# The last layer's down projection by token rows, with the final norm done along rows

## The chip, the cores and the metric

The kernel runs on one core of a Trainium2 chip. The metric is the device time of one execution in microseconds (us). An execution is profiled separately: the profiler records every instruction of every engine, and the pages quoted here come from one such execution. The engines are called as the profile calls them: PE (TensorE) multiplies matrices, PEld is its loading of the stationary operand, DVE is VectorE, ACT is ScalarE, POOL is GpSimd, SP is SyncE, which here only issues transfers. A q behind a name (SPq, ACTq, POOLq) is that engine's instruction queue.

## The reference

Two layers of a token mixer (three branches, merged by gates) and a gated MLP with a causal convolution, then one RMS norm. For this case only the end matters. S = 512 tokens, D = 1024 features, 2816 hidden columns, all float32:

```python
for l in range(DEPTH):                      # DEPTH = 2
    ...
    x = x + jnp.sum(gates * proj, axis=2) @ w_out[l]
    x = x + conv_ffn(rmsnorm(x, norm2_g[l]), ffn_w_up[l], ffn_conv_w[l], ffn_conv_b[l], ffn_w_down[l])
return rmsnorm(x, final_g)

def rmsnorm(x, g):
    y = x * lax.rsqrt(jnp.mean(x * x, axis=-1, keepdims=True) + EPS) * g
```

`conv_ffn` multiplies by the up weights (1024 to 5632 columns), convolves over three tokens, forms silu(gate) * value (2816 columns) and multiplies by the down weights (2816 to 1024).

## The kernel before

**Layout.** Activations are kept feature-major: a tile has 128 features on the partitions and 512 tokens along the row, so the residual x is eight tiles `x[0..7]`. A matrix product keeps float32 accuracy by three products: each factor is split into a high part (a cast by ACT) and a low part (a subtraction by DVE), and `mm3` (L146 to L157, with the products at L151) issues high x low, high x high and low x high into one PSUM bank. Weights arrive as units of 128 x 512 numbers, 256 KB, by SP's queue into three raw buffers (`load`, L117); `part` (L125) splits them: ACT casts at L134 (tile `sh` or `wh`), DVE subtracts at L135 (`sl` or `wl`). Units are loaded and split ahead of their use: `AHEAD` allows two to five units, by the pool that the split unit goes to. There are 31 "u" buffers, 16 "r" buffers and 39 "f" buffers of 256 KB, and PSUM has two groups of four banks, `acc` and `sm`. A unit feeds 12 products of 512 columns.

**Order.** A scheduler sets each engine's order from the program as written, except where `keep_in_program_order` (`po` in the listing) or `pin` holds it.

**The last layer's end.** `wout` (L1010) computes the residual's tiles one after the other (L1018), splits their normalised form for the up projection and sums their squares (`norm_sq`, L213). `ffn_up` (L1025) takes 22 pairs of columns (gate and value), 24 products each column: DVE evacuates the bank at L1040, ACT and DVE convolve (L1042 to L1044), ACT's tanh and two DVE steps form the activation, and its split at L1052 and L1053 gives the tile pair `ah` (high, low), which goes to an "f" buffer for the first 39 tiles and to an "r" buffer for the last five. `ffn_down` (L1057) takes one output tile of 128 features at a time: 22 slices of the weights are stationary, the activations' 512 tokens move, 66 products in all, then DVE adds half the product to the residual (L1067; the activations are kept doubled) and the squares are summed (L215, L217). In the last layer this goes for tiles 0 to 6.

`finish` (L1078) does tile 7 in two halves of 256 tokens, 66 products of 256 columns each, and interleaves the final norm with them. The squares were added up over tiles 0 to 6 per partition; tiny products with a column of ones sum them over the partitions (L1138 for those tiles, L1107 for tile 7). ACT takes the root (L1109), DVE the reciprocal (L1110); that gives a factor for each token, on the partitions. TensorE turns the factors into rows (L1118), and then eight tiles are multiplied by gain and factor (L1132 on DVE; in the second half two of them at L1130 on GpSimd, with the gain put in earlier by ACT) and stored in 16 pieces of 128 KB (L1133), by SP's and ACT's queues. The first half's multiplications and stores run under the second half's products; the second half's stand alone after the last product.

**Turning.** `turned` (L220) is used by the token mixer for another tile: DVE transposes 32 x 32 blocks (L222), the result is stored to DRAM (`trip`, L227), and four transfers of 64 KB read it back so that rows and columns of blocks are exchanged too (L225).

Of the kernel before, what the change touches and what calls it, by code (L numbers as in the profile page):

```python
# [32 lines left out]
for _n, _w in (("n1", 8), ("mu", 14), ("kk", 4), ("ka", 4), ("a0", 4), ("w0", 4), ("rk", 4), ("lg", 4), ("lb", 4),  # L33
               ("n2", 8), ("cw0", 44), ("cw1", 44), ("cw2", 44), ("cb", 44), ("fg", 8), ("sg", 4), ("sb", 4)):
    PC[_n] = _o
    _o += _w
# [11 lines left out]
class Emit:  # L48
# [251 lines left out]
    def run(self):  # L300
        nc, tc, a, V = self.nc, self.tc, self.a, self.nc.vector
# [9 lines left out]
        st = self.norm_new()  # L311
# [713 lines left out]
    def ffn_up(self, l, st):  # L1025
        nc, V, A = self.nc, self.nc.vector, self.nc.scalar
        nt = [0]

# [28 lines left out]
    def ffn_down(self, l, act, x, st):  # L1057
        nc, V = self.nc, self.nc.vector
        if l < L - 1:
            self.load_pc(l + 1)  # L1060
        xd = []
        for m in range(8):
            if l == L - 1 and m == 7:
                break
            ps = self.acc()
            self.matF(ps, ("wdn", l, m, 0), act)
            V.scalar_tensor_tensor(x[m], ps, 0.5, x[m], op0=MUL, op1=ADD)  # L1067
            if l < L - 1:
                self.norm_z(st, x[m], "n1")
            self.norm_sq(st, x[m])  # L1070
            if l < L - 1:
                d = self.dp.tile([128, 512], F32, name=self.nm("xd"))
                nc.gpsimd.dma_start(d, x[m])
                xd.append(d)
        return x, xd


    def finish(self, l, act, x, acc):  # L1078

        nc, V, A, T = self.nc, self.nc.vector, self.nc.scalar, self.nc.tensor  # L1080
        self.pool = "u"
        w = [self.unit("wdn", l, 7, k * 512, min(512, DFF - k * 512)) for k in range(6)]
        po = self.tc.keep_in_program_order
        pt = self.sm((128, 4))
        hs = [slice(0, 256), slice(256, 512)]
        pss, gx = [self.acc((128, 256)) for _ in range(2)], []

        def prod(h, k0, k1):
            for k in range(k0, k1):
                ks = slice(k % 4 * 128, k % 4 * 128 + 128)  # L1090
                (wh, wl), (xh, xl) = w[k // 4], act[k]
                self.mm3(pss[h], (wh[:, ks], wl[:, ks]), (xh[:, hs[h]], xl[:, hs[h]]), k == 0, k == NFF - 1)

        def square(h):

            sq = self.u((128, 256), n="sq")
            for e in range(2):
                es = slice(128 * e, 128 * e + 128)
                xi = x[7][:, 256 * h + 128 * e:256 * h + 128 * e + 128]
                po(V.scalar_tensor_tensor(xi, pss[h][:, es], 0.5, xi, op0=MUL, op1=ADD))  # L1100
                po(A.activation(sq[:, es], xi, AF.Square))
            return sq

        def stats(h, sq):
            for e in range(2):
                c = 2 * h + e
                po(T.matmul(pt[:, c:c + 1], sq[:, 128 * e:128 * e + 128], self.c("ones"), start=False, stop=True, skip_group_check=True))  # L1107
            ms, rs = self.small((128, 2), "ms"), self.small((128, 2), "rs")
            po(A.activation(ms, pt[:, 2 * h:2 * h + 2], AF.Sqrt, scale=1.0 / D, bias=self.c("eps")))  # L1109
            po(V.reciprocal(rs, ms))  # L1110
            return rs

        def out(h, rs):

            pb = [self.sm((128, 256)) for _ in range(1 + h)]
            for p in pb:
                for e in range(2):
                    po(T.transpose(p[:, 128 * e:128 * e + 128], rs[:, e:e + 1].to_broadcast([128, 128]), self.c("ident")))  # L1118
            return pb

        def scale(h, pb):

            if gx:
                pbs = self.u((128, 256), n="pbs")
                po(A.copy(pbs, pb[1]))
            order = (0, 2, 1, 3, 4, 5, 6, 7) if gx else range(8)
            for j in order:
                t = self.u((128, 256), n="o")
                if gx and j < 2:
                    nc.gpsimd.tensor_tensor(t, gx[j], pbs, op=MUL)  # L1130
                else:
                    po(V.scalar_tensor_tensor(t, x[j][:, hs[h]], self.p("fg", j), pb[0], op0=MUL, op1=MUL))  # L1132
                (nc.scalar if j in (1, 4, 6) else nc.sync).dma_start(self.a["out"][:, j, hs[h]], t)  # L1133

        self.pin = True
        prod(0, 0, 8)
        for c in range(NC):
            po(T.matmul(pt[:, c:c + 1], acc[:, 128 * c:128 * c + 128], self.c("ones"), start=c == 0, stop=False, skip_group_check=True))  # L1138
        prod(0, 8, NFF)
        sq = square(0)  # L1140
        prod(1, 0, 4)
        rs = stats(0, sq)
        prod(1, 4, 8)
        pb = out(0, rs)
        scale(0, pb)
        for j in range(2):
            t = self.u((128, 256), n="gx")
            A.activation(t, x[j][:, hs[1]], AF.Copy, scale=self.p("fg", j))
            gx.append(t)
        prod(1, 8, NFF)  # L1150
        rs = stats(1, square(1))
        scale(1, out(1, rs))

# [55 lines left out]
def _layout(i):  # L1209
    wall, wdn, pcols = [], [], []  # L1210
    for l in range(L):
        w = i["w_in"][l]
# [8 lines left out]
        for j in range(3):  # L1221
# [4 lines left out]
        wdn.append(_chunks(i["ffn_w_down"][l]))  # L1226
# [3 lines left out]
             "cb": i["ffn_conv_b"][l], "fg": i["final_g"], "sg": i["sg_ln_g"][l], "sb": i["sg_ln_b"][l]}  # L1230
# [5 lines left out]
        "wall": np.stack(wall), "wdn": np.stack(wdn), "pcols": np.stack(pcols),  # L1236
# [30 lines left out]
```

## Time and profile before

| what | us |
|---|---|
| median of 3 runs (lowest to highest) | 1719.29 (1718.9 to 1719.91) |
| the profiled execution's own time | 1719.05 |
| its span, first to last instruction | 1717.3 |
| PE busy | 1703.7 |
| DVE busy | 1152.7 |
| ACT busy | 772.5 |
| POOL busy | 147.3 |
| last layer's up projection | about 1358 to 1585 |
| last layer's down projection, tiles 0 to 6 | about 1585 to 1690 |
| tile 7 and the final norm | 1690 to 1717.3 |

Times within the profile count from the start of the span. A row of a group of instructions gives line, engine, operation, output and inputs with their shapes, the count, the busy time and the mean in ns, and then the idle time ahead of them with what ended it. A row of the timeline gives start, duration, and in brackets the idle time before it. The granted clock of TensorE was 0.998 of full speed in the mean. The chip's other cores are not used.

### The profile page before, as it was taken

What the parts mean: (1) busy time and instruction counts of PE and PEld (TensorE: products, weight loads), DVE (VectorE), ACT (ScalarE), POOL (GpSimd) and SP (SyncE); (2) the same over time, 40 slices, a digit from 0 to 9 for tenths busy, and PEclk for the clock granted to TensorE, in tenths of its full rate; (3) what the DMA queues carried; (4) which work ended last, traced back from release to release, by engine and by line L of the source; (5) the groups of instructions that cost most, each with busy time, mean ns of one, the idle gap of its engine ahead of it and who ended that gap; (6) DMA issues with size and microseconds to landing.
All of it is one profiled execution on the core that took longest, in us unless ns stands there. A gap on an engine that the chain in (4) does not pass through costs nothing.

```text
span 1717.3 us, 27555 instructions
## 1 busy us (share of the span) xinstructions
PE 1703.7 (99%) x10368; PEld 1397.7 (81%) x10368; DVE 1152.7 (67%) x1980; ACT 772.5 (45%) x1308; POOL 147.3 (9%) x163
## 2 busy tenths in 40 slices
PE   9999999999999999999999999999999999999997
PEld 7888777788888888888888887778888888888887
DVE  6887745578569777753377886565776787776433
ACT  6563433554255444343265634345433544443322
POOL 2121000013200000000021300000131000000000
PEclk9999999999999999999999999999999999999999
DMA  5236543625443333243332365445254333322332
GB/s 180 87 110 204 172 150 123 184 87 171 149 148 98 98 97 95 72 118 110 115 111 80 122 215 173 132 143 171 89 189 146 125 98 97 99 98 65 107 96 83
DMA packets 132324, 214.89 MB, mean 125 GB/s; under 512 B 16352, under 2 KB 39136, under 8 KB 132192
## 3 DMA queue, kind: packets, MB, share of 16 engines
q1 hardware_dynamic: 117344, 180.67, 34.4%
q10 hardware_dynamic: 10368, 17.78, 2.9%
q0 software_dynamic: 4480, 14.68, 2.6%
q8 instruction: 81, 1.33, 0.3%
q14 instruction: 51, 0.42, 0.1%
HBM read 185.81 MB, written 27.26 MB: 124 GB/s over the span
## 4 chain that ended last, share of the span: by engine, by line
PE 87%; DMA 5%; DVE 4%; ACT 1%; issue 1%; SPq 1%; ACTq 0%; POOL 0%; DVEq 0%; POOLq 0%
PE acc L151 81%; DMA wr<-wall 2%; PE sm L639 2%; DVE wl L135 1%; PE sm L884 1%; PE sm L546 1%; SPq L225 1%; DMA tr<-qkt 1%; DMA tr<-bkT 1%; DMA ws<-sgw 1%; PE sm L989 0%; DMA bkS<-tr 0%; DMA tab<-rot 0%; DVE cs L765 0%; ACT sh L134 0%
## 5 line engine op out<-in xcount | busy, mean ns | idle before, releaser
L151 PE MATMUL acc<-hi,sh 128*128 128x512 f32 x1108 | 431.8, 390 | 0.0
L151 PE MATMUL acc<-lo,sh 128*128 128x512 f32 x1108 | 431.6, 390 | 0.0
L151 PE MATMUL acc<-hi,sl 128*128 128x512 f32 x1108 | 430.5, 390 | 0.0
L134 ACT CAST sh<-wr 128x512 fp32r<-128x512 f32 (+1 forms) x389 | 236.2, 611 | 403.1 <-PE acc L151 305.6
L135 DVE TENSOR_TENSOR sl<-wr,sh 128x512 fp32r<-128x512 f32 (+1 forms) x389 | 262.4, 678 | 185.6 <-PE acc L151 91.5
L151 PEld LDWEIGHTS acc<-lo,sh 128*128 128x128 f32 x1108 | 208.0, 188 | 43.9 <-issue 0.9
L151 PEld LDWEIGHTS acc<-hi,sh 128*128 128x128 f32 x1108 | 208.0, 188 | 43.4 <-issue 0.3
L151 PEld LDWEIGHTS acc<-hi,sl 128*128 128x128 f32 x1108 | 208.0, 188 | 43.4 <-DVE gth L1004 0.3
L151 PE MATMUL acc<-lo,wh 128*128 128x512 f32 x588 | 231.9, 394 | 0.7 <-ACT wh L134 0.4
L151 PE MATMUL acc<-hi,wl 128*128 128x512 f32 x588 | 230.4, 392 | 0.7 <-DVE wl L135 0.6
L151 PE MATMUL acc<-hi,wh 128*128 128x512 f32 x588 | 229.3, 390 | 0.0
L135 DVE TENSOR_TENSOR wl<-wr,wh 128x512 fp32r<-128x512 f32 x195 | 137.9, 708 | 125.2 <-ACT wh L134 122.3
L151 PE MATMUL acc<-ah,sh 128*128 128x512 f32 (+1 forms) x748 | 219.5, 377 | 0.0
L134 ACT CAST wh<-wr 128x512 fp32r<-128x512 f32 x195 | 120.4, 619 | 214.5 <-PE acc L151 145.9
L151 PEld LDWEIGHTS acc<-ah,sh 128*128 128x128 f32 x748 | 137.6, 188 | 25.8
L151 PE MATMUL acc<-ah,sl 128*128 128x512 f32 (+1 forms) x374 | 140.8, 376 | 0.0
L151 PEld LDWEIGHTS acc<-hi,wl 128*128 128x128 f32 x588 | 110.4, 188 | 27.5 <-DVE wl L135 3.8
L151 PEld LDWEIGHTS acc<-lo,wh 128*128 128x128 f32 x588 | 110.3, 188 | 25.5 <-ACT wh L134 1.1
L151 PEld LDWEIGHTS acc<-hi,wh 128*128 128x128 f32 x588 | 110.4, 188 | 22.3 <-issue 0.2
L1040 DVE TENSOR_TENSOR fu<-acc,rsF 128x512 f32<-128x512 f32 x88 | 60.7, 690 | 70.2 <-PE acc L151 70.1
L1042 ACT ACTIVATE cv<-fu,pc 128x512 f32<-128x512 f32 x88 | 71.6, 816 | 41.3 <-DVE fu L1040 37.0
L151 PEld LDWEIGHTS acc<-ah,sl 128*128 128x128 f32 x374 | 70.4, 188 | 12.8
(295 smaller groups left out, 2079.1 us busy)
## 6 DMA issues: line engine op xcount, KB each, us to landing
wr<-wall SPq DMA_DIRECT2D x488, 256.0 KB, 2.6
wr<-wdn SPq DMA_DIRECT2D x80, 256.0 KB, 2.7
gd<-gth ACTq DMA_DIRECT2D x48, 256.0 KB, 3.0
gth<-gd POOLq DMA_DIRECT2D x48, 256.0 KB, 3.5
tr<-bkT SPq DMA_DIRECT2D x16, 256.0 KB, 3.2
bkS<-tr SPq DMA_DIRECT2D x128, 32.0 KB, 2.4
tr<-vT SPq DMA_DIRECT2D x8, 256.0 KB, 2.6
Vt<-tr SPq DMA_DIRECT2D x32, 64.0 KB, 2.3
```

Of the source, the lines that this page charges most:

```text
L134: self.kept(self.nc.scalar.copy(hi[:, :n], raw[:, :n]))
L135: self.kept(self.nc.vector.tensor_tensor(lo[:, :n], raw[:, :n], hi[:, :n], op=SUB))
L151: i = self.nc.tensor.matmul(*x, **y)
L225: q.dma_start(o[32 * f:32 * f + 32, :].rearrange("d (a x) -> d a x", a=4), d[:, f * 128:f * 128 + 128].rearrange("(a d) x -> d a x", d=32))
L546: i = T.matmul(pK[hv[1 - h], j, :], bk[hv[h], c, 1, :], x[hv[h], c, :], start=True, stop=True)
L639: po(T.matmul(o, l, r, start=start, stop=True, skip_group_check=True))
L884: po(T.matmul(X[h][:, i, :], lhsT, rhs, start=new[h], stop=stop, skip_group_check=True))
L1040: V.tensor_tensor(u, ps, self.rsF, op=MUL)
L1042: A.activation(t, u, AF.Identity, scale=self.p("cw2", j), bias=self.p("cb", j))
```

## The change

Three things are done in another way in the last layer.

The residual is turned to token-major during the up projection. Ahead of each of the columns i = 1, 3, ... 15, `turned` is called for one of the eight residual tiles, with DVE's transpose, and with GpSimd's queue for one store of 256 KB and four reads of 64 KB. Both the intermediate tile `xT` and the result `xt` are "r" buffers; the eight results are held to the end.

The down projection is done by token rows (`last`, in place of `ffn_down` and `finish`). Slices of 128 tokens of the activations are stationary, rows of the weights (128 hidden columns by 512 output features) move, in a layout `wdt` made on the host, as the reordering of the weights was before. The first 512 features are accumulated in the four `acc` banks, one for each chunk of 128 tokens, weight unit by weight unit. The second 512 features go to the four `sm` banks; there the last six units (`KEPT`) stay split in "u" buffers, and the products that need them are done chunk by chunk, 18 for each, so that the chunks end one after another.

The final norm runs along rows. A token is now a partition, so ACT sums the squares itself while squaring (`accum_out`), and no product is needed for the sums or for the factors. The first half's squares and its multiplication by the gain (by GpSimd; the gain `fgr` is loaded as a row and repeated on all partitions) run under the second half. For each chunk the second half's squares are summed, ACT takes the root with the first half's sum as its bias, DVE takes the reciprocal, ACT multiplies the first half by the factor and DVE the second by factor and gain, and two stores of 256 KB go out by ACT's and SP's queues. The last chunk's second half is added, squared and summed in three steps, of 256, 128 and 128 features, the first two going into the bias. The output is token-major; before, the host turned it.

The sums of squares of the last layer's tiles (`norm_sq` in `ffn_down`) fall away, and `ffn_down` serves layer 0 alone. The constants lose the eight gain columns.

```diff
+KEPT = 6
...
-            act = self.ffn_up(l, st)
-            st = self.norm_new()
-            x, xd = self.ffn_down(l, act, x, st)
+            act = self.ffn_up(l, st, x if l == L - 1 else None)
             if l == L - 1:
-                self.finish(l, act, x, st["acc"])
+                self.last(act)
             else:
+                st = self.norm_new()
+                x, xd = self.ffn_down(l, act, x, st)
...
         for i in range(NFF):
+            if x and i % 2 == 1 and i < 17:
+                o = self.r(n="xt")
+                self.turned(o, self.r(n="xT"), x[i // 2], nc.gpsimd)
+                self.xt.append(o.rearrange("p (a c d) -> p c a d", c=4, d=32))
...
-    def finish(self, l, act, x, acc):
...
+    def last(self, act):
+        nc, V, A, P, po = self.nc, self.nc.vector, self.nc.scalar, self.nc.gpsimd, self.tc.keep_in_program_order
+        fg = [self.u(n="fg") for _ in range(2)]
+        for h in range(2):
+            nc.sync.dma_start(fg[h], self.a["fgr"][:, 512 * h:512 * h + 512].to_broadcast([128, 512]))
+        ss, bias = self.small((128, NC), "fss", 1), self.small((128, NC), "fbi", 1)
+        self.pin = True
+        def prod(ps, k, c, w):
+            cs = slice(128 * c, 128 * c + 128)
+            ah, al = act[k]
+            self.mm3(ps, (ah[:, cs], al[:, cs]), w, k == 0, k == NFF - 1)
+        def add(y, ps, j, c):
+            b = slice(j % 4 * 128, j % 4 * 128 + 128)
+            q = lambda t: t[:, b].rearrange("p (a d) -> p a d", d=32)
+            return V.scalar_tensor_tensor(q(y), q(ps), 0.5, self.xt[j][:, c], op0=MUL, op1=ADD)
+        def square(y, s):
+            return A.activation(self.u(n="sq")[:, 0:y.shape[1]], y, AF.Square, accum_out=s)
+        self.pool = None
+        pss = [self.acc() for _ in range(NC)]
+        for k in range(NFF):
+            w = self.unit("wdt", 0, k, 0)
+            for c in range(NC):
+                prod(pss[c], k, c, w)
+        ya = []
+        for c in range(NC):
+            y = self.u(n="ya")
+            for j in range(4):
+                add(y, pss[c], j, c)
+            square(y, ss[:, c:c + 1])
+            P.tensor_tensor(y, y, fg[0], op=MUL)
+            ya.append(y)
+        V.tensor_scalar(bias, ss, 1.0 / D, 1e-6, op0=MUL, op1=ADD)
+        pss = [self.sm() for _ in range(NC)]
+        for k in range(NFF - KEPT):
...
+        self.pool = "u"
+        ws = [self.unit("wdt", 0, k, 512) for k in range(NFF - KEPT, NFF)]
+        def factor(s, b):
+            rs = self.small((128, 1), "frs")
+            po(A.activation(rs, s, AF.Sqrt, scale=1.0 / D, bias=b))
+            po(V.reciprocal(rs, rs))
+            return rs
+        for c in range(NC - 1):
+            for k, w in enumerate(ws, NFF - KEPT):
+                prod(pss[c], k, c, w)
+            y, s = self.u(n="yb"), self.small((128, 1), "fs1")
+            for j in range(4, 8):
+                po(add(y, pss[c], j, c))
+            po(square(y, s))
+            rs = factor(s, bias[:, c:c + 1])
+            po(A.activation(ya[c], ya[c], AF.Copy, scale=rs))
+            nc.scalar.dma_start(self.a["out"][c, :, 0:512], ya[c])
+            po(V.scalar_tensor_tensor(y, y, rs, fg[1], op0=MUL, op1=MUL))
+            nc.sync.dma_start(self.a["out"][c, :, 512:1024], y)
...
+        for j0, j1 in ((4, 6), (6, 7), (7, 8)):
+            for j in range(j0, j1):
+                po(add(y, pss[c], j, c))
+            s = self.small((128, 1), f"fs{j0}", 1)
+            po(square(y[:, 128 * j0 - 512:128 * j1 - 512], s))
+            if j1 < 8:
+                po(V.scalar_tensor_tensor(b, s, 1.0 / D, b, op0=MUL, op1=ADD))
...
```

The rows below are instructions in the order in which an engine runs them: the line, the operation, the output and the inputs, and the output's shape. The same statement has a higher line number in the changed kernel: one more up to `wout` (L135 is L136 there), six more behind the new lines of `ffn_up` (L1040 is L1046).

First DVE at its end, before (`xi` is the residual's tile 7 or another one, `sm` the turned factors, `pc` holds the gain) and in the change (`sm` a bank with products, `xt` a turned residual tile, `yb` the output row, `fs` sums of squares, `fbi` the bias, `frs` the factor):

```order
L1100 SCALAR_TENSOR_TENSOR xi_13568<-acc_16461,xi_13568 128x128 x2
L1110 RECIPROCAL rs_16648<-ms_16647 128x2
L1132 SCALAR_TENSOR_TENSOR o_16662<-xi_13333,pc_7489,sm_16651 128x256
L1132 SCALAR_TENSOR_TENSOR o_16668<-xi_13380,pc_7489,sm_16651 128x256
L1132 SCALAR_TENSOR_TENSOR o_16671<-xi_13427,pc_7489,sm_16651 128x256
L1132 SCALAR_TENSOR_TENSOR o_16674<-xi_13474,pc_7489,sm_16651 128x256
L1132 SCALAR_TENSOR_TENSOR o_16677<-xi_13521,pc_7489,sm_16651 128x256
L1132 SCALAR_TENSOR_TENSOR o_16680<-xi_13568,pc_7489,sm_16651 128x256
```

```order
L1098 SCALAR_TENSOR_TENSOR yb_16613<-sm_16205,xt_14511 128x128
L1098 SCALAR_TENSOR_TENSOR yb_16613<-sm_16205,xt_14708 128x128
L1154 SCALAR_TENSOR_TENSOR fbi_15768<-fs_3456_16634,fbi_15768 128x1
L1098 SCALAR_TENSOR_TENSOR yb_16613<-sm_16205,xt_14905 128x128
L1154 SCALAR_TENSOR_TENSOR fbi_15768<-fs_3458_16639,fbi_15768 128x1
L1098 SCALAR_TENSOR_TENSOR yb_16613<-sm_16205,xt_15102 128x128
L1130 RECIPROCAL frs_16647<-frs_16647 128x1
L1156 SCALAR_TENSOR_TENSOR yb_16613<-yb_16613,frs_16647,fg_15764 128x512
```

Where six multiplications of 256 columns followed one reciprocal, four adds stand with two small updates between them, and one multiplication of 512 columns ends the list; each update stands ahead of the next add.

Next DVE at the end of the up projection in the changed kernel (`fu` is the evacuated column, L1046; `cv` its convolution; `ah` a part of the activation; `sl` the low part of a weight unit, L136):

```order
L1046 TENSOR_TENSOR fu_15706<-acc_15675,rsF_13681 128x512
L1059 TENSOR_TENSOR ah_15672<-fth_15667,ah_15671 128x512
L136 TENSOR_TENSOR sl_15679<-wr_15625,sh_15678 128x512
L1049 SCALAR_TENSOR_TENSOR cv_15708<-fu_15706,pc_7489,cv_15708 128x511
L1050 SCALAR_TENSOR_TENSOR cv_15708<-fu_15706,pc_7489,cv_15708 128x510
L1046 TENSOR_TENSOR fu_15749<-acc_15712,rsF_13681 128x512
```

The unit's low part `sl_15679`, which the last column's second half uses, stands between the evacuations of the last two columns.

Last DVE where `wout` ends and the up projection begins, before and in the change (`sq` the running sum of squares, `lo` and `hi` split tiles, `xT` the first transposed tile):

```order
L210 SCALAR_TENSOR_TENSOR lo_13609<-xi_13568,pc_7489,hi_13608 128x512
L217 TENSOR_TENSOR sq_13612<-sq_13565,sq_13612 128x512
L135 TENSOR_TENSOR sl_13770<-wr_13704,sh_13769 128x512
L144 TENSOR_TENSOR lo_13616<-sq_13612,hi_13615 128x512
L135 TENSOR_TENSOR sl_13788<-wr_13722,sh_13787 128x512
```

```order
L211 SCALAR_TENSOR_TENSOR lo_13609<-xi_13568,pc_7489,hi_13608 128x512
L223 STREAM_TRANSPOSE xT_13761<-xi_13240 128x4x4x32
L218 TENSOR_TENSOR sq_13612<-sq_13565,sq_13612 128x512
L145 TENSOR_TENSOR lo_13616<-sq_13612,hi_13615 128x512
L136 TENSOR_TENSOR sl_13779<-wr_13704,sh_13778 128x512
```

The first transpose stands ahead of the last sum of squares, on which the factors of the second norm wait.

More of the change, by code (lines that the diff above doesn't have):

```diff
@@ L1075, in ffn_down @@
+            xd.append(d)
         return x, xd
-    def finish(self, l, act, x, acc):
-        nc, V, A, T = self.nc, self.nc.vector, self.nc.scalar, self.nc.tensor
-        self.pool = "u"
[L1082 to L1110, printed above, removed]
-            return rs
[L1113 to L1152, printed above, removed]
@@ new lines, in last @@
+    def last(self, act):
[32 more added lines that the diff above has]
+        for k in range(NFF - KEPT):
+            w = self.unit("wdt", 0, k, 512)
+            for c in range(NC):
+                prod(pss[c], k, c, w)
+        self.pool = "u"
+        ws = [self.unit("wdt", 0, k, 512) for k in range(NFF - KEPT, NFF)]
[3 more added lines that the diff above has]
+            po(V.reciprocal(rs, rs))
+            return rs
+        for c in range(NC - 1):
+            for k, w in enumerate(ws, NFF - KEPT):
+                prod(pss[c], k, c, w)
+            y, s = self.u(n="yb"), self.small((128, 1), "fs1")
[7 more added lines that the diff above has]
+            nc.sync.dma_start(self.a["out"][c, :, 512:1024], y)
+        c, y, b = NC - 1, self.u(n="yb"), bias[:, NC - 1:]
+        for k, w in enumerate(ws, NFF - KEPT):
+            prod(pss[c], k, c, w)
+        for j0, j1 in ((4, 6), (6, 7), (7, 8)):
[5 more added lines that the diff above has]
+                po(V.scalar_tensor_tensor(b, s, 1.0 / D, b, op0=MUL, op1=ADD))
+        rs = factor(s, b)
+        po(V.scalar_tensor_tensor(y, y, rs, fg[1], op0=MUL, op1=MUL))
+        nc.sync.dma_start(self.a["out"][c, :, 512:1024], y)
+        po(A.activation(ya[c], ya[c], AF.Copy, scale=rs))
+        nc.scalar.dma_start(self.a["out"][c, :, 0:512], ya[c])
@@ L1209, in _layout @@
 def _layout(i):
[L1210 removed]
+    wall, pcols = [], []
     for l in range(L):
```

29 lines of the change are left out of this document (12 added, 17 removed).

## The prediction

> **What bounds the kernel now.** I read the spans first, then busy time by stage, then the chain of waits, then the end alone. The first two tell which engine has no room.
>
> ```profile
> PE 1703.7 (99%) x10368; PEld 1397.7 (81%) x10368; DVE 1152.7 (67%) x1980; ACT 772.5 (45%) x1308; POOL 147.3 (9%) x163
> 1358.00:1585.00 227.00, 227.00 (x1003) 188.04 (x1002) 177.97 (x274) 107.31 (x167) 0.00 (x0) 1.00 0.29 90
> 1585.00:1690.00 105.00, 105.00 (x466) 86.98 (x465) 39.63 (x62) 31.32 (x54) 0.00 (x0) 1.00 0.36 102
> ```
>
> The window rows give length, then busy time of PE, weight loads, DVE, ACT and POOL, the clock, and the DMA share. The last layer's up projection is 1358 to 1585, its down projection follows. TensorE has no gap in either, at full clock; VectorE is busy for 78% and 38%, GpSimd never. So work taken from or added to any other engine there is worth nothing until TensorE has to wait for it. What counts is TensorE's own stream, and the time after its last product:
>
> ```profile
> 1196.01 5.44 PE acc L151 x24
> 1357.93 334.94 PE acc L151 x1489
> 1692.87 0.79 PE sm L1138 x8
> 1693.66 6.58 PE acc L151 x54
> 1700.24 0.34 PE sm L1107 x4
> 1700.58 1.53 PE acc L151 x12
> 1702.11 0.22 PE sm L1118 x2
> 1702.33 5.04 PE acc L151 x42
> 1689.84 0.40 PE L151 MATMUL acc<-ah,sh 128*128 128x256 f32 x2
> 1707.08 0.28 PE L151 MATMUL acc<-ah,sl 128*128 128x256 f32 x1
> ```
>
> The chain from the statistics of norm2 to 1707.4 is TensorE alone. Its last 132 products are 256 columns wide, at 5.04 / 42 = 0.120 us each, and three blocks of tiny products (sums of squares, turning the factors) cost 0.79 + 0.34 + 0.22 = 1.35 us between them. A 512-wide product costs 5.44 / 24 = 0.2267 us; that row is a stage in which activations are already the stationary side and weights the moving one, as the change has it. The span ends at 1717.3, so 9.94 us follow the last product's end at 1707.36.
>
> **The TensorE term.** Before the last tile nothing changes in number: seven of eight column tiles are 462 products, and the changed kernel's 528 are the same 462 plus 66. From 1689.84 to 1707.36 the old kernel runs 132 half-width products and the three blocks, 17.52 us. The new one runs 66 products of 0.2267 there: 65 starts are 14.74, and the last one lasts 0.39 by any row of its width, so 15.13. That is **-2.4 us**. Of it 1.35 are the removed blocks, the rest is mostly 132 x 0.120 = 15.84 against 66 x 0.2267 = 14.96. The Trainium skill (TensorE: Matmul & The Clock Gate, Back-to-back issue gap) gives 262 cycles for 256 columns and 518 for 512, so two halves would cost 2.5 ns more than one whole; the rows here show 13 ns. By the page the gain would be 1.35 + 0.17 = 1.5 us and not 2.4; I go by the rows.
>
> **Added in the up projection: eight turns of the residual.** Each is one VectorE transpose and five transfers in GpSimd's queue.
>
> ```profile
> L222 DVE STREAM_TRANSPOSE qkt<-ro 128x512 f32<-128x512 f32 x8 | 5.6, 695 | 0.0
> L1001 POOL DMA_DIRECT2D gth<-gd x48: 538/538/757, 365.3 to 1303.4; - x48
> DMA to landing us min/median/max: 2.8/3.5/6.2
> 1579.88 0.69 DVE L1040 TENSOR_TENSOR fu<-acc,rsF 128x512 f32<-128x512 f32 x1 [0.61 <-PE acc L151]
> 1585.12 0.62 PE L151 MATMUL acc<-ah,sh 128*128 128x512 f32 x2
> ```
>
> 8 x 0.70 = 5.6 us of VectorE against 227 - 178 = 49 idle: hidden. 40 issues of 0.54 on an idle GpSimd: hidden. What is not free is buffers. The 16 "r" buffers now hold eight turned tiles to the end, so weight casts wait for the buffer that was freed last. Two places are tight. First, the order has the split of the last up column's second weight unit behind the evacuation (L1040) of the column before. Call the last column's end E, 1585.12 in the trace; columns are 24 x 0.2267 = 5.44 apart. The evacuation of the column before started at 1579.88, so E - 5.24; then three VectorE steps of 0.6 to 0.7, so the split is done by E - 3.3, and the unit's low part is wanted from E - 2.3. Second, the down projection now opens four PSUM banks at once: the fourth is wanted nine products after E, at E + 2.04, and the last evacuation, 0.2 behind E and 0.69 long, is done by E + 0.9. About 1.1 us are left at both, so I take **0**, with +0.7 (one VectorE step out of place) as the upper bound. Nothing there can be gained, since TensorE waits for nothing today. The first turn also stands ahead of the last sum of squares and delays norm2's factors by 0.7 us; TensorE has four columns of products before it needs an evacuated bank, so 0.
>
> In the first half's drain, 16 adds on VectorE and four GpSimd products by the gain run under TensorE's second half. GpSimd and VectorE do get in each other's way:
>
> ```profile
> 1271.02 1.29 POOL L1007 TENSOR_TENSOR gth<-gth,gth 128x512 f32<-128x512 f32 x1 [9.75 <-DVE gth L1004]
> 1271.57 1.29 DVE L1007 TENSOR_TENSOR gth<-gth,gth 128x512 f32<-128x512 f32 x1
> ```
>
> A VectorE step of 0.69 took 1.29 beside GpSimd's. Here the weights are two units, 5.4 us, ahead, and one such hold of 0.6 plus seven adds (under 2 us) fit: 0, and if that cover failed, 0.6 for each of four products. The Trainium skill (SBUF — State Buffer, Who interferes with whom) says that a VectorE instruction with two SBUF inputs contends with a GpSimd one that reads SBUF; the row agrees.
>
> **The tail.** What happens today after the last product, and what each step of the new chain costs:
>
> ```profile
> 1707.39 0.49 DVE L1100 SCALAR_TENSOR_TENSOR xi<-acc,xi 128x128 f32<-128x128 f32 x2 [1.80 <-PE acc L151]
> 1707.78 0.51 ACT L1101 ACTIVATE sq<-xi 128x128 f32<-128x128 f32 x2 [5.73 <-DVE xi L1100]
> 1708.78 0.26 ACT L1109 ACTIVATE ms<-sm,con 128x2 f32<-128x2 f32 x1 [0.50 <-PE sm L1107]
> 1709.08 0.17 DVE L1110 RECIPROCAL rs<-ms 128x2 f32<-128x2 f32 x1 [1.20 <-ACT ms L1109]
> 1709.83 2.44 DVE L1132 SCALAR_TENSOR_TENSOR o<-xi,pc,sm 128x256 f32<-128x256 f32 x6 [0.59 <-PE sm L1118]
> L1100 DVE SCALAR_TENSOR_TENSOR xi<-acc,xi 128x128 f32<-128x128 f32 x4 | 1.0, 285 | 8.2 <-PE acc L151 8.2
> L955 DVE TENSOR_SCALAR bve<-bmv 128x1 f32<-128x1 f32 x8 | 1.2, 150 | 0.1
> L1044 DVE SCALAR_TENSOR_TENSOR cv<-fu,pc,cv 128x510 f32<-128x510 f32 x88 | 65.6, 746 | 1.2
> L1101 ACT ACTIVATE sq<-xi 128x128 f32<-128x128 f32 x4 | 1.0, 302 | 13.2 <-DVE xi L1100 13.2
> L215 ACT ACTIVATE sq<-xi 128x512 f32<-128x512 f32 x31 | 19.3, 622 | 11.6 <-DVE xi L1067 11.6
> L320 ACT COPY ms<-rst 128x1 f32<-128x1 f32 x1 | 0.2, 191 | 0.0
> 1711.00:1711.50 0.50, 0.00 (x0) 0.00 (x0) 0.50 (x3) 0.00 (x0) 0.50 (x2) 0.87 0.59 211
> 1712.50:1713.00 0.50, 0.00 (x0) 0.00 (x0) 0.00 (x0) 0.00 (x0) 0.00 (x0) 0.50 0.99 338
> 1714.50:1714.75 0.25, 0.00 (x0) 0.00 (x0) 0.00 (x0) 0.00 (x0) 0.00 (x0) 0.50 0.86 311
> 1710.34 2.71 SPq L1133 DMA_DIRECT2D out<-o  x5
> gd<-gth ACTq DMA_DIRECT2D x48, 256.0 KB, 3.0
> SPq L1258 <- DMA out<-o: 1.8, 5, 0.6
> ```
>
> Today: two adds, squares, the sums by TensorE, root, reciprocal, factors turned (usable at 1709.83), six products of 0.41 on VectorE beside two on GpSimd, eight stores of 128 KB. The first store is issued at 1710.34; at 338 GB/s, the 211 of 1711.0 to 1711.5 mean a start near 1711.19, 0.85 later. Bytes flow until 1714.75, and the span ends 2.55 after that.
>
> New, counted from the last product's end T. The last chunk's quarter sums go in three steps; the first two are added into the bias of the root before the third.
> - Two adds 0.03 + 0.49. Square over 256 columns: between the rows of 128 (0.30) and 512 (0.62) 0.41, after a hop of 0.09 (add started 1707.39, 0.285 long, square 1707.78). Bias on VectorE 0.03 + 0.16, as a 1-column step takes 0.15. So 1.21.
> - Add 0.285, hop 0.09, square 0.30, bias 0.19: 0.87. Add, hop, square again: 0.675. So 2.75.
> - Root 0.05 + 0.26, reciprocal 0.03 + 0.17: the factor is ready at 3.26.
> - VectorE's two-factor product over 512 columns 0.03 + 0.75 (L1044's shape), beside ScalarE's product: 4.04.
> - Store issued 0.10 later, first bytes after 0.85; two stores of 256 KB at 340 GB/s are 1.54; end 2.55 after: 9.08.
>
> What no row shows is what ScalarE takes to hand out a square's sum; it enters three times. Below: 0, since a gain is excluded. Above: a whole one-column step of ScalarE, 0.19. Back-to-back steps of ScalarE overlap by about 0.1 (two squares of 0.302 took 0.51), so some of that 0.19 is start-up that would not be paid again: I take 0.10. The tail is then 9.08 + 0.30 = 9.4 against 9.94: **-0.55**, between -0.85 and -0.3. The chunks before the last have 18 products, 4.08 us, for a like chain of 2.8 plus 0.8, so their stores are gone before it. The root's one function-table load falls under chunk 0's or 1's products, where before it fell under the second half's.
>
> **Sum.** 1719.05 (profiled execution; its span of 1717.3 and 1.75 around it) - 2.4 - 0.55 = 1716.1. The median of the runs, 1719.29, is 0.24 above that execution, so the forecast is 1716.1 + 0.2 = **1716.3**, 3.0 faster. 0.2%, about what a measurement here can tell from no change, is 3.4 us: faster begins under 1715.85, slower over 1722.7.
>
> **Rivals.**
>
> *A cheaper tail.* Summing while squaring costs nothing (-0.3), and the end after the last bytes shrinks, since SP today waits five times, 1.8 us in all, for stores at the close (L1258), and the new kernel has two stores left there, not eight. A fifth to a fourth of that 1.8 saved is 0.4. For: the row. Against: 256 KB land in 3.0, 128 KB in less, so the last landing itself is not earlier. 1716.3 - 0.7 = 1715.6: faster.
>
> *The new chain gives it back.* Six hops between VectorE and ScalarE at 0.1 more each, sums at 0.19 (+0.27), and one VectorE step out of place at the change from up to down (+0.7): +1.6, 1717.9. For: about 1.1 us of slack in two places. Against: the measured hop of 0.09 is of the same kind.
>
> *Width gives nothing.* Two half products cost one whole: TensorE's term is 1.5 instead of 2.4, 1717.2. That is the page's rule. Against: 5.04 over 42.
>
> *GpSimd's trips hold the weight casts* (slower). An "r" buffer with a turned tile is freed only when its store in GpSimd's queue has landed; a weight cast that wants it waits in ScalarE's queue, and behind it stand the activations of the column (L1042, L1048, L1052), then VectorE, then TensorE. From the transpose to the products that need the weight there are four half columns, 2.72 x 4 = 10.9; transpose, issue, cast, split and the hops take some 4.6. So up to a landing of about 6.2 nothing happens. GpSimd's loads land in 2.8 to 6.2, median 3.5, and its queue now holds stores and reads in turn, of which reads wait for the store. Each us beyond stalls TensorE up to eight times: at a landing of 7, 8 x 0.8 = 6.4, hence 1716.3 + 6.4 = 1722.7, and 8 would give 1730. It decides from about 6.6 on. Against: 3.5 is the median, and the 6.2 belongs to a stage in which other stores ran.
>
> **Chances.** Forecast 0.40; cheaper tail 0.32; given back 0.10; width nothing 0.04; trips hold casts 0.14. Faster by over 0.2% 0.32, within 0.54, slower 0.14. The range leaves out most of the last case, and at the lower end what a tail still 0.8 cheaper than its rival would give: 1714.8 to 1720. The forecast's own, from the tail's and the tight places' bounds (-0.3 and +0.25, +0.7): 1716.0 to 1717.3.
>
> **What will show it.** In the chain of waits, no blocks of tiny products in the last layer's end, and a row of products with activations as the stationary side at 0.2267 each; if they cost 0.23 or more, the TensorE term is wrong. In the windows, TensorE without a gap from the end of wout to the last product; a gap near the end of the up projection means that the split or the evacuation is late; gaps of equal size every second column mean that trips hold casts, and then ScalarE's weight casts wait for a store, and GpSimd's store lands after 6.6. The last product should end 2.4 earlier. In the end's timeline, the factor 3.3 to 3.8 after that, the last store issued by 4.5, the span's end 9.4 after it. A tail over 10 or a first gap over 1 us makes the forecast wrong.

## The result and the profile after

The changed kernel took 1728.07 us (median of 6 runs, 1725.95 to 1729.76) against 1719.1 before (6 runs, 1716.69 to 1719.91): a ratio of 1.0054, 95% interval 1.0043 to 1.0065. It is slower by about 9 us; 3.0 faster was forecast, and the range ended at 1720.

The end of the chain of waits of the changed kernel's profiled execution (span 1727.1), in order of time: start, duration, what, and how many.

```profile
1369.03 0.23 PE sm L258
1369.25 0.23 PE sm L259
1369.48 288.16 PE acc L152 x1264
1657.64 61.45 PE sm L152 x264
1719.09 0.02 issue
```

TensorE still works without a gap, and 8.0 us follow the last product (1727.1 - 1719.1) in place of 9.94. So the tail became shorter, by more than was forecast. Two things are wrong elsewhere. The statistics of norm2, which the edit puts only three products later, come at 1369.03 in place of 1357.48: 11.6 us, of which three products explain 0.7. All that lies ahead of them is code that the diff does not touch. And the second half of the down projection is 264 products in 61.45 us, 0.2328 each, where 0.2267 was forecast.

The loss is thus a rate, and a window in the first layer's down projection shows it best, since its code is the same in both kernels and TensorE is never idle in it. The columns are length, then busy time and count of PE, weight loads, DVE, ACT and POOL, clock, DMA share and GB/s; first the kernel before, then the changed one.

```profile
750.00:850.00 100.00, 100.00 (x443) 82.81 (x442) 40.15 (x63) 33.95 (x58) 3.80 (x7) 1.00 0.42 124
```

```profile
750.00:850.00 100.00, 100.00 (x431) 80.71 (x430) 37.89 (x60) 31.88 (x54) 3.26 (x6) 1.00 0.40 119
```

443 products start in 100 us before, 431 after; both are busy all the time at a granted clock of 1.00. (Busy time says nothing here: each record lasts about 0.39 and they overlap. The count in a full window, or the time between starts, is the rate.) In other stages, such as 600 to 700 (the first layer's up projection), they start 442 and 443. Over all products of 512 columns, waits left out, the mean time between starts in the kernel before is 0.2267 to 0.227, with or without an operand in an "f" buffer. In the changed kernel it is 0.227 for those with both operands outside the "f" buffers, and 0.2333 for those that read an "f" buffer, whether as the moving operand (1585 such times) or as the stationary one (472).

What moved is those buffers. A partition's memory is handed out pool after pool: constants, weights, "u", "r", small tiles, and then the pools that hold the mixer's tiles and the "f" buffers. Each tile is rounded up to 32 bytes. The change has eight gain columns less in two constant tiles (968 bytes in place of 1000, 32 less each after rounding, 64 in all) and nine more slots of 32 bytes for its sums, biases and factors (`fss`, `fbi`, `fs1` and `frs` twice, `fs4`, `fs6`, `fs7`: 288 bytes). The "f" buffers move by 224 bytes:

```text
address in the built program     before    after
"u" buffers, first               41792     41792     64 modulo 256 in both
"r" buffers, first              105280    105280     64 modulo 256 in both
"f" buffers, first              146496    146720     64 and 32 modulo 256
```

The first theory was that an operand must begin at a multiple of 64 bytes. By the listed program 2100 products read exactly one operand from an "f" buffer (1628 moving, 472 stationary); at 0.0066 each that is 13.9 us. With the 2.4 that TensorE's term saves, and a tail 1.9 shorter, the sum is 9.6 slower, about what was measured.

### The profile page after: what moved, and what is told of

The parts are those of the page before. It is cut to its first block, busy times and chain, and to the rows that moved or that the text cites. A ratio compares the mean times of both kernels' runs of the same rounds, so it can differ in the third digit from the quotient of the medians.

```text
span 1727.1 us, 27357 instructions
## 1 busy us (share of the span) xinstructions
PE 1713.8 (99%) x10280; PEld 1392.3 (81%) x10280; DVE 1155.4 (67%) x1994; ACT 774.4 (45%) x1316; POOL 173.8 (10%) x205
## 4 chain that ended last, share of the span: by engine, by line
PE 92%; DMA 4%; DVE 2%; issue 1%; ACT 1%; SPq 1%; POOL 0%; ACTq 0%; POOLq 0%
PE acc L152 82%; PE sm L152 4%; PE sm L640 2%; DMA wr<-wall 2%; PE sm L885 1%; PE sm L547 1%; DVE wl L136 1%; DMA bkS<-tr 0%; PE sm L990 0%; ACT wh L135 0%; DMA tr<-qkt 0%; DMA con<-con 0%; DMA x<-xT 0%; SPq L226 0%; DMA tr<-bkT 0%
## 5 line engine op out<-in xcount | busy, mean ns | idle before, releaser
L135 ACT CAST sh<-wr 128x512 fp32r<-128x512 f32 (+1 forms) x347 | 212.2, 615 | 364.6 <-PE acc L152 271.1
L136 DVE TENSOR_TENSOR sl<-wr,sh 128x512 fp32r<-128x512 f32 (+1 forms) x347 | 235.9, 682 | 146.9 <-ACT sh L135 81.6
L136 DVE TENSOR_TENSOR wl<-wr,wh 128x512 fp32r<-128x512 f32 x233 | 165.2, 710 | 185.6 <-ACT wh L135 182.6
L135 ACT CAST wh<-wr 128x512 fp32r<-128x512 f32 x233 | 143.9, 619 | 282.8 <-PE acc L152 184.3
L152 PE MATMUL acc<-ah,sh 128*128 128x512 f32 x352 | 110.5, 395 | 0.0
L1046 DVE TENSOR_TENSOR fu<-acc,rsF 128x512 f32<-128x512 f32 x88 | 60.6, 689 | 56.6 <-PE acc L152 56.5
L1049 DVE SCALAR_TENSOR_TENSOR cv<-fu,pc,cv 128x511 f32<-128x511 f32 x88 | 65.8, 748 | 20.9 <-ACT cv L1048 20.3
L152 PEld LDWEIGHTS acc<-ah,sh 128*128 128x128 f32 x352 | 66.1, 188 | 15.8
L152 PE MATMUL acc<-wl,hi 128*128 128x512 f32 x192 | 78.4, 408 | 0.0
```

The source lines that it names most:

```text
L135: self.kept(self.nc.scalar.copy(hi[:, :n], raw[:, :n]))
L136: self.kept(self.nc.vector.tensor_tensor(lo[:, :n], raw[:, :n], hi[:, :n], op=SUB))
L152: i = self.nc.tensor.matmul(*x, **y)
L1046: V.tensor_tensor(u, ps, self.rsF, op=MUL)
L1049: V.scalar_tensor_tensor(t[:, 1:], u[:, :511], self.p("cw1", j), t[:, 1:], op0=MUL, op1=ADD)
```

## The experiments

Ratios are to the kernel before, run on the same chip in the same session; its median was 1720.66, 1718.5 and 1718.61 us in the three sessions.

**32 bytes more.** The changed kernel with one unused small tile:

```diff
         ss, bias = self.small((128, NC), "fss", 1), self.small((128, NC), "fbi", 1)
+        P.memset(self.small((128, 1), "pad", 1), 0.0)
```

> The changed kernel with one more tile of 32 bytes in the pool of small tiles (GpSimd sets it to zero once; it is not used). It moves the f buffers, which lie behind that pool, from an address of 32 modulo 64 back to a multiple of 64. Theory (address): 2084 products of 512 columns that read an f buffer lose 0.0067 us each, 13.9 in all, so about 1714.2 in place of 1728.07, and every stage runs at 0.2267 per product. Rival (the new stage's work or its transfers slow TensorE): no difference, 1728. Rival (any shift cures it): 1714 here and in the kernel with 64 bytes too.

1716.39 us, ratio 0.9979 (0.9970 to 0.9988). One unused tile of 32 bytes turns a kernel that is 0.54% slower into one that is 0.21% faster. The window and the chain of this kernel:

```profile
750.00:850.00 100.00, 100.00 (x443) 82.81 (x442) 39.92 (x63) 34.25 (x58) 3.79 (x7) 1.00 0.42 123
```

```profile
1362.42 286.72 PE acc L152 x1264
1649.14 59.85 PE sm L152 x264
1708.99 0.02 issue
```

443 products again, and the same 264 products of the second half take 59.85 in place of 61.45, 0.2267 each. The new stage itself is not slow.

**64 bytes more.** The same with a tile of 64 bytes (`(128, 16)`).

> The same with a tile of 64 bytes: the f buffers move, but stay at 32 modulo 64. Theory (address): no difference, 1728, and 0.233 per product where an f buffer is read. Rival (any shift of the f buffers or one more instruction cures it): 1714.

1730.58 us, ratio 1.0056 (1.0042 to 1.0069), as the unpadded kernel's 1.0054; the "f" buffers lie at 96 modulo 256 and their products take 0.2333. A shift alone cures nothing.

**The kernel before, with 32 bytes more.** One unused small tile in `finish`, set by GpSimd.

> The kernel before, with one more tile of 32 bytes in the pool of small tiles and nothing else: its f buffers move to 32 modulo 64. Theory (address): 2065 products of 512 columns read an f buffer, 13.8 us more, about 1733; the 118 products of 256 columns with an f buffer may add up to 0.8. Rival (the address is not the cause): 1719.

1732.82 us, ratio 1.0064 (1.0051 to 1.0077): 11 us slower by an unused tile. The 13.8 expected lies just outside the interval, 8.8 to 13.2; the products that read an "f" buffer take 0.2332 in this run's trace. The window:

```profile
750.00:850.00 100.00, 100.00 (x431) 80.54 (x430) 37.86 (x64) 31.41 (x53) 3.24 (x6) 1.00 0.40 117
```

So the change's slowness can be had without the change, and taken from it by 32 bytes.

**The last chunk in one step.** The tail's three steps showed a cost that the prediction had taken from the edit unasked: the chain from the first add to the factor is 2.16 us for chunk 2 and 3.21 for the last one, since each step waits for the one before.

```diff
-        for j0, j1 in ((4, 6), (6, 7), (7, 8)):
-            for j in range(j0, j1):
-                po(add(y, pss[c], j, c))
-            s = self.small((128, 1), f"fs{j0}", 1)
-            po(square(y[:, 128 * j0 - 512:128 * j1 - 512], s))
-            if j1 < 8:
-                po(V.scalar_tensor_tensor(b, s, 1.0 / D, b, op0=MUL, op1=ADD))
+        s = self.small((128, 1), "fs1")
+        for j in range(4, 8):
+            po(add(y, pss[c], j, c))
+        po(square(y, s))
```

> The changed kernel with the last chunk's second half added, squared and summed in one step as the other chunks are, in place of three. It has three small tiles fewer, so its f buffers lie at a multiple of 64. Theory: as the kernel with 32 bytes more (about 1714.2), less what three serial steps cost beyond one: chunk 2 took 2.16 us from its first add to its factor, the last chunk 3.21, so 1.05 less, about 1713.2; the factor is ready 2.2 after the last product. Rival (the steps hide work, as they were meant to): equal to the kernel with 32 bytes more, or slower.

1727.61 us, ratio 1.0037 (1.0024 to 1.0049). The tail (from the end of the last product to the end of the span) was 6.9, about 1.0 shorter, as expected; the total was not. Its "f" buffers lie at 146624, a multiple of 64, and still their products take 0.2324 (stationary) and 0.2328 (moving), and the window shows the slow rate:

```profile
750.00:850.00 100.00, 100.00 (x432) 80.61 (x431) 37.62 (x61) 31.91 (x54) 3.24 (x6) 1.00 0.40 117
```

The theory of 64 bytes fell. What this kernel shares with the slow ones, and not with the fast ones, is that the "f" buffers (192 modulo 256) and all others (64 modulo 256) lie differently within 256 bytes.

**Everything moved by 32 bytes.** The kernel before with 32 bytes ahead of its first tile:

```diff
+        nc.gpsimd.memset(self.cp.tile([128, 8], F32, name="pad"), 0.0)
         self.con = self.cp.tile([128, NCC], F32, name="con")
```

> The kernel before with 32 bytes put in front of all its pools: every tile moves from 64 to 96 modulo 256, so the two operands of a product still lie alike. The kernel with the single step (f buffers at 192, others at 64 modulo 256) ran at 0.2328 per product although 192 is a multiple of 64, so the rule of the first four runs is wrong as stated. Theory (relative): what counts is that a product's moving and stationary operands lie at the same place modulo 256; then no difference, 0.2267 everywhere, 1719 to 1721. Rival (absolute: an operand must lie at 64 modulo 256, or at some other fixed place): every product of 512 columns costs 0.233, about 6800 of them 0.0067 each, 45 us more, about 1765.

1718.77 us, ratio 1.0001 (0.9992 to 1.0010), 0.227 per product everywhere. The "f" buffers are at 146528, the very address that made the kernel before 11 us slower, and cost nothing now that all other buffers lie at 96 modulo 256 too. The window:

```profile
750.00:850.00 100.00, 100.00 (x443) 82.81 (x442) 40.15 (x64) 33.68 (x58) 3.79 (x7) 1.00 0.41 123
```

An address is not good or bad by itself; what counts is how a product's two operands lie to each other.

**A sweep in one kernel.** The changed kernel with the 32 bytes, and the high parts of the weights at changing places:

```diff
-            hi, lo = [self.wp.tile([128, 512], F32R, name=self.nm(t), tag=t, bufs=3) for t in ("wh", "wl")]
+            hi = self.wp.tile([128, 528], F32R, name=self.nm("wh"), tag="wh", bufs=3)
+            if not self.nsw:
+                self.nc.gpsimd.memset(self.wp.tile([128, 16], F32, name="pad", tag="pad", bufs=1), 0.0)
+            lo = self.wp.tile([128, 512], F32R, name=self.nm("wl"), tag="wl", bufs=3)
+            o = self.nsw // 3 * 5 % 16
+            hi = hi[:, o:o + 512]
+            self.nsw += 1
```

> The changed kernel with the 32 bytes, whose weights' high parts (three buffers, the stationary operand in the layers, the moving one in the last down projection) are put at changing places, 4 to 60 bytes further unit by unit, in buffers that lie at 64, 128 and 192 modulo 256; all else stays at 64. Theory (relative): products of a unit at 64 run at 0.2267, those at any other place slower, by up to 0.0067, alike for moving and stationary operand. Rival (only multiples of 64 or 128 count): 0.2267 at 128 or 192 too. Rival (only the f buffers matter): 0.2267 everywhere.

One run, 1726.21 us. Mean time from a product's start to the next one's, from the trace, by where the operand that is not at 64 modulo 256 lies:

```text
place modulo 256     weights stationary       weights moving
64, next alike       0.2270 (4200 products, both operands at 64)
68 to 124            0.2318 (342)             0.2331 (222)
128                  0.2322 (40)              -
132 to 188           0.2322 (342)             0.2336 (212)
192                  0.2341 (40)              -
196 to 252           0.2320 (341)             0.2327 (224)
```

No other range of places comes near 0.2270, multiples of 64 and 128 included, and it is the same for either operand and for buffers that are not "f" buffers. It is not a plain function of the distance: single places go from 0.2265 (stationary at 196, 16 products) to 0.2374 (moving at 212, 8 products). The slowness is not confined to the misplaced product either. A product with both operands at 64 is slow too (0.2318, 538 of them) if the next one's stationary operand lies elsewhere, and so is one with both at 64 that stands between two whose moving operand lies elsewhere (0.2319, 311). So the table says that misplaced operands cost time, not which product of a group pays.

**One step, all buffers alike.** The single step with 128 bytes more in the small tiles, so that the "f" buffers are at 64 modulo 256.

> The kernel with the last chunk in a single step, with 128 bytes more in the pool of small tiles, so that the f buffers go from 192 to 64 modulo 256 like all others. Theory (relative or absolute, 256): all products at 0.2267, ratio to the kernel before 0.9979 (that of the changed kernel with 32 bytes) less 1.05 us, so about 0.9973; the factor is ready 2.2 after the last product. Rival (the last chunk's steps hide work): 0.9979 or above. Rival (the place is not the cause): 1.0037 as before.

1713.13 us, ratio 0.9970 (0.9960 to 0.9979); the kernel at 192, which differs in nothing but 128 unused bytes and the instruction that sets them, had 1.0037. The end of its timeline:

```profile
1707.50 0.39 PE L152 MATMUL sm<-sh,ah 128*128 128x512 f32 x1
1707.93 0.88 DVE L1099 SCALAR_TENSOR_TENSOR yb<-sm,xt 128x128 f32<-128x128 f32 x4 [1.13 <-PE sm L152]
1708.84 0.63 ACT L1102 ACTIVATE sq<-yb 128x512 f32<-128x512 f32 x1 [2.01 <-DVE yb L1099]
1709.38 0.19 ACT L1102 ACTIVATION_READ_ACCUMULATOR sq<-yb 128x1 f32 x1
1709.60 0.29 ACT L1130 ACTIVATE frs<-fs,fbi 128x1 f32<-128x1 f32 x1
1709.92 0.16 DVE L1131 RECIPROCAL frs<-frs 128x1 f32<-128x1 f32 x1 [1.11 <-ACT frs L1130]
```

The factor is there 2.2 after the last product, and the span ends 6.91 after it (7.92 with three steps).

**No kept units** (`KEPT = 0`, three steps, the 32 bytes).

> The changed kernel with the 32 bytes and no kept units: the second half's four banks end within 2 us of each other. Theory (the chunks' staggering hides three chunks' evacuation and scaling): VectorE's 1.8 per chunk (four adds 0.88, reciprocal 0.16, product 0.75) stand three times more behind the last product, so about 5 us later, ratio 1.001. Rival (the stores' end sets the tail): under 2 us later.

1721.84 us, ratio 1.0025 (1.0016 to 1.0034). The tail is 15.8 us, 7.9 longer than with six kept units, where 5 was expected: the chunks follow each other at 2.86 (adds at 1706.75, 1709.61 and 1712.47 in the profile), not at VectorE's 1.8, because VectorE also waits about 1.1 in each for the square and the root. Part of it is also the root's function-table load of 1.28, which ends behind the last product here; in the kernel with six kept units and the 32 bytes it starts at 1698.43, over 10 us ahead of the last product's end.

```profile
1704.26 1.28 ACT L1130 ACT_TABLE_LOAD   x1
1705.56 0.29 ACT L1130 ACTIVATE frs<-fs,fbi 128x1 f32<-128x1 f32 x1
1706.75 0.87 DVE L1099 SCALAR_TENSOR_TENSOR yb<-sm,xt 128x128 f32<-128x128 f32 x4
```

The products end at 1704.60. So chunk 1's adds begin 2.15 behind them, and two more chunks at 2.86 make the 7.9.

**The last products and stores in halves** (from the best kernel so far: product by the factor, then store, for 256 columns at a time).

> The kernel with the last chunk in a single step and all buffers at 64 modulo 256 (ratio 0.9970), with the last chunk's two products by the factor cut into halves of 256 columns, each stored as soon as it is there. Theory (what follows the factor is product, store, landing in a row): the first store is issued about 0.35 earlier, the bytes take 1.4 either way, so the span ends 0.3 to 0.4 earlier after the last product (6.9 becomes 6.5 to 6.6), ratio 0.9968, which the timing can't tell from 0.9970. Rival (each store has a landing of its own that ends the kernel, and four cost more than two): 6.9 or longer.

1712.21 us, ratio 0.9962 (0.9949 to 0.9974). The tail is 6.7 against 6.9, about 0.25 less; the ratios' intervals overlap, so by the time alone the two can't be told apart. The first store is issued 0.26 earlier, but the bytes go at 338 to 340 GB/s, where the kernel with whole stores of 256 KB shows 369 to 389:

```profile
1707.50:1708.00 0.50, 0.00 (x0) 0.00 (x0) 0.00 (x0) 0.00 (x0) 0.00 (x0) 1.00 1.01 340
1708.00:1708.50 0.50, 0.00 (x0) 0.00 (x0) 0.00 (x0) 0.00 (x0) 0.00 (x0) 0.53 0.97 338
```

This is the lowest median of the versions run, 0.38% under the kernel before by the ratio; the kernel with whole stores (0.9970) and the one below (0.9964) lie within its interval.

**The turns in SP's queue** (`nc.sync` for `nc.gpsimd` in `ffn_up`, from the single step with all buffers alike).

> The same kernel as the one with ratio 0.9970, with the eight turns' stores and reads in SP's queue, where the weights are loaded, in place of GpSimd's. Theory (weights are loaded and split three units, 8 us, ahead, and a trip blocks the queue for its store's landing, about 3, and five issues, about 2): no gap at TensorE, ratio 0.997. Rival (the queue is the tight place, which is why GpSimd's was taken): gaps of some us at TensorE in the up projection, ratio 0.998 to 1.005.

1712.93 us, ratio 0.9964 (0.9950 to 0.9977): no loss. SP's own waits and the whole stage in one window, of this kernel:

```profile
SPq L226 <- DMA tr<-xT: 15.8, 7, 3.0
...
1360.00:1590.00 230.00, 230.00 (x1017) 190.39 (x1016) 185.95 (x286) 107.92 (x170) 0.00 (x0) 1.00 0.34 111
```

SP does stand still for the stores of the turns, 15.8 us in seven waits, and TensorE notices nothing. The queue has room: in the same stretch SP stands still ten times as long, 150.5 us, until DVE has split a unit and its raw buffer is free. Moving the turns to GpSimd's queue was not needed.

## Why the prediction was wrong

**The step that failed** is the sentence "Before the last tile nothing changes in number", and the price of 0.2267 beside it. The count was right; the price of each product, here and in the stages that the diff does not touch, was taken to be a property of the shape. In these runs it holds only where the operands lie alike modulo 256, as all of them do in the kernel before; in the changed kernel 2100 products cost 0.2333. The prediction costed nine small tiles and a narrower constant tile at nothing without naming them, and they decided the result: 13.9 us by the count, 12.9 by the two ratios (1.0054 and 0.9979). No rival covered it, and the range of 1714.8 to 1720 could not hold it.

With that cause taken away (the kernel with 32 bytes more), the other steps can be checked one by one.

- **TensorE's term, forecast -2.4.** From the first product of the last down projection to the end of the last: 122.24 us before (1585.12 to 1707.36), 119.84 with the 32 bytes. That is -2.40. By the Trainium skill (TensorE: Matmul & The Clock Gate, Back-to-back issue gap), whose 262 cycles for 256 columns and 518 for 512 make two half products cost little more than one whole, it would have been 1.5, an estimate; the measured 2.40 does not agree.
- **The up projection, forecast 0, upper bound +0.7.** The first tight place has no slack instead of 1.1: the split of the last column's second unit ends as TensorE wants it. In the kernel with 32 bytes, with the idle time in brackets:

```profile
1585.99 0.69 DVE L136 TENSOR_TENSOR sl<-wr,sh 128x512 fp32r<-128x512 f32 x1
1586.73 0.19 PEld L152 LDWEIGHTS acc<-hi,sl 128*128 128x128 f32 x1 [0.34 <-DVE sl L136]
```

  The cost is 0.2 (two products start 0.08 and 0.11 late). It varies within this set: the changed kernel itself has none, the first kernel with the single step 0.27.
- **The tail, forecast -0.55.** It was 9.95 and became 7.92: -2.0, so the rival "a cheaper tail" was the better account, and even that gave 1.25. The chain to the factor was well sized, 3.24 against 3.26 + 0.30: reading out a sum costs 0.19, but it starts before the square ends, and the next add starts before the bias has ended.

```profile
1710.47 0.31 ACT L1102 ACTIVATE sq<-yb 128x128 f32<-128x128 f32 x1 [0.42 <-DVE yb L1099]
1710.69 0.19 ACT L1102 ACTIVATION_READ_ACCUMULATOR sq<-yb 128x1 f32 x1
1710.90 0.16 DVE L1155 SCALAR_TENSOR_TENSOR fbi<-fs,fbi 128x1 f32<-128x1 f32 x1 [0.47 <-ACT sq L1102]
1710.98 0.28 DVE L1099 SCALAR_TENSOR_TENSOR yb<-sm,xt 128x128 f32<-128x128 f32 x1
1713.04 0.33 SPq L1158 DMA_DIRECT2D out<-yb  x1
```

  What was mis-sized lies behind it. The store is issued at 1713.04, 4.06 after the last product (4.44 by the sum). The bytes then go faster, and the close is shorter:

```profile
1714.00:1714.50 0.50, 0.00 (x0) 0.00 (x0) 0.00 (x0) 0.00 (x0) 0.00 (x0) 0.50 1.00 389
1714.50:1715.00 0.50, 0.00 (x0) 0.00 (x0) 0.00 (x0) 0.00 (x0) 0.00 (x0) 0.50 1.00 385
1715.00:1715.50 0.50, 0.00 (x0) 0.00 (x0) 0.00 (x0) 0.00 (x0) 0.00 (x0) 0.50 0.50 185
1715.50:1716.90 1.40, 0.00 (x0) 0.00 (x0) 0.00 (x0) 0.00 (x0) 0.00 (x0) 0.50 0.00 0
```

  Two stores of 256 KB ran at 385 to 389 GB/s where eight of 128 KB ran at 338, and the span ends about 1.65 after the last byte in place of 2.55: 0.9 of the tail's surprise.
- **The sum.** -2.4 + 0.2 - 2.0 is -4.2; the ratio 0.9979 (0.9970 to 0.9988) is -3.6 with an interval of -5.2 to -2.1. The forecast of -3.0 lies in that interval, which says nothing for its parts: TensorE's term was right, the tail was off by more than 1.4, and an interval 3 us wide can't show that. And it describes this kernel, not the changed one.
- **GpSimd's trips** do not hold the casts. With the 32 bytes, the stores in GpSimd's queue land in a median of 2.3 and the reads in 2.9 (at most 3.2 and 4.7), under the 6.2 that the sum allowed, and TensorE has no gap that repeats with the turns:

```profile
tr<-xT POOLq DMA_DIRECT2D x8, 256.0 KB, 2.3
xt<-tr POOLq DMA_DIRECT2D x32, 64.0 KB, 2.9
```

- **GpSimd beside VectorE** in the first half's drain showed in no wait of TensorE; that part was forecast at 0 and was 0.
- **The three steps of the last chunk** were forecast as they are (2.75 to the last sum) but not questioned: all of the chunk's sums are complete with its last product, so there is nothing for a first step to overlap with. One step is 1.0 us shorter.

The tests planned in the prediction did name the sign that appeared, "if they cost 0.23 or more, the TensorE term is wrong". It was looked for in the new stage alone; the stages before it cost three quarters of the loss.

## What to carry to other kernels

In a kernel that TensorE bounds, compare the time between starts of equal products stage by stage before arguing about the edit; here, a few per cent in stages that were not edited were the sign that operands had moved. List where the buffers lie, and keep the moving and the stationary operands alike modulo 256: round each pool of small tiles up to 256 bytes, so that a tile added in one place does not cost 13 us in another. When steps are cut to overlap with something, name what is still running at that point.

## What the runs showed of the hardware that was not expected

Two operands of a float32r product of 512 columns (128 rows, 128 stationary columns) that lie differently modulo 256 bytes raise its cadence from 0.2267 to 0.2333 us when the distance is 32 bytes either way, and to about 0.2326 when it is 128. Shifts by 256, and a common shift of everything by 32, cost nothing. The records' duration of a weight load stays at 0.188. The Trainium skill (SBUF — State Buffer, Operand start alignment) says that an operand may begin at any multiple of its element size and adds that this is about legality, with nothing timed; all places here ran, and the runs put a price on them.

How it comes about is open. That a product with both operands in place is slow when the next stationary operand is not would fit a moving stream that meets the load of the next weights in the memory. But two groups of the sweep do not fit it: a product whose own stationary operand is misplaced while the next one's is not (0.2319, 561 products), and a product in place between two with a misplaced moving operand (0.2319, 311). So this account is not shown. Whether both operands in "f" buffers are fast among differently placed neighbours was not settled: there are only 24 such products in the changed kernel, at 0.2298. No run here tells more.
